# The gate projection as seven half-size products, summed in DRAM, beside the heads of an encoder layer

## The chip, the cores and the metric

The kernel runs on one core of a Trainium2 chip. The metric is the device time of one execution in microseconds (us). Three executions of the kernel before gave a median of 1530.08 us (1529.75 to 1530.29).

## The reference, cut to what matters

One layer with S = 1024 rows and D = 1024 columns. The heads, the pooling branch and the gates all read the same normalized input h:

```python
h = rmsnorm(x, g_mix[l])
z = h @ w_in[l]                      # pooling channels | q | k | v
...
qn = head_rmsnorm(q, g_q) * (HEAD_DIM ** -0.5)
kn = head_rmsnorm(k, g_k)
s = jnp.einsum('bqhid,bkhid->bihqk', qblk, kn)
...
gates = jax.nn.sigmoid(h @ w_gate[l] + b_gate[l])        # 1024 x 2048
merged = (gates[..., :D_MODEL] * (y_pool @ w_branch_pool[l])
          + gates[..., D_MODEL:] * (y_attn @ w_branch_attn[l]))
x = x + merged @ w_out[l]
h2 = rmsnorm(x, g_ffn[l])
x = x + jnp.square(jax.nn.relu(h2 @ w_up[l])) @ w_down[l]
```

## The kernel before, in words

Every float32 operand of a large product is split into a high and a low part (`split`: ScalarE makes the high part at L131, VectorE or GpSimd the low part at L132), and each product is three matmuls (`mm3`, L138 to L140: high by high, high by low, low by high). The transposed input hT lies in SBUF as four pairs of 128-row blocks (kp) by two halves of the rows (th) by high and low: sixteen tiles of 128 x 1024 words, in the pools `hp0` (th 0) and `hp1` (th 1).

The heads run as a software pipeline over 64 steps g (8 heads of 8 row blocks). The string `O` gives the stages and their lag in steps: A projects q, k and v (`stage_qkv`, 24 matmuls 128 x 384 into z), B normalizes q and k (`stage_prep`: ScalarE squares, VectorE sums, GpSimd raises to -1/2 at L271, VectorE scales, and GpSimd multiplies k's half by the weights `ggh` at L710), C transposes q and k and splits them (`stage_qkT`), D makes the scores and the softmax (`stage_scores`), E transposes the probabilities (`stage_aT`), F multiplies by v (`stage_pv`), H sums squares (`stage_ssq`), R writes the norms of a finished head to `r_dram` (`stage_norm`, L884), and W loads and splits the next head's weights `wqkv` (eight tiles, each free only when the old head's last block has used it).

TensorE's idle places in this pipeline are filled with *units* of other work, which `fillers` yields: a unit is half a column block (th) of the gates (`gate_cols`, 24 matmuls 128 x 512 into g, `fill_proj`) or of the pooling channels. One unit is traced for every two steps (`F_PACE` 0.5) from step 4 on, 34 of them in the loop and the last 6 behind it. Weights for the units go through two landing tiles `fr` and four split tiles `fw`; a gate unit's result gets its bias on ScalarE (L387) and is written to `g_dram` from ScalarE's queue (256 KB).

The order on each engine's queue is fixed when the program is built: a planner goes through the traced instructions by priority (tracing order) and by its own cost estimates, and an instruction waits on its engine until all its operands are there, with everything behind it on that engine waiting too. `tc.issue_after` holds an instruction behind another one of the same queue.

Behind the heads, stage `bp` multiplies the pooled rows by `w_branch_pool` (192 matmuls; its operands ypT lie in the `hp0` tiles that hT leaves), and stage `ba` multiplies the head outputs yT by `w_branch_attn` (384 matmuls). yT is loaded from `y_dram` and scaled by the rows of `r_dram`, so its last block needs the last head's norm. During `bp` `w_out_sums` also reads 4 MB of w_out and writes 4 MB of sums (`wos`, `w_sum`), in tiles whose room the heads' pool leaves. `gate` (L229, L230) then loads the gates and applies the sigmoid.

Of the kernel before, what the change touches and what calls it, by code (L numbers as in the profile page):

```python
# [48 lines left out]
ORDER = [(w[0], int(w[1:])) for w in O.split()]  # L49
G_FIRST, G_Z = 13, 13  # L50
F_FROM, F_PACE, F_UNITS = 4, 0.5, 34

# [11 lines left out]
def encoder_kernel(  # L64
# [86 lines left out]
    def w_tile(shape, name, i, dt=F32R):  # L151
        return wpool.tile(shape, dt, tag=f"W{int(i)}", name=name, bufs=N_W // 2)

    def fw_tile(shape, name, dt=F32R):
        return fwpool.tile(shape, dt, tag="fw", name=name)

    def fo_tile(name):
        return fp.tile([P, 528], F32, tag="fo", name=name, bufs=N_FO)
# [68 lines left out]
    def gate(gts, c):  # L227
        for gt, c0, c1 in gts:
            nc.sync.dma_start(gt, g_dram[c * P : (c + 1) * P, c0:c1])  # L229
            nc.scalar.activation(gt, gt, AF.Sigmoid, bias=zero)  # L230

# [32 lines left out]
    p_dram = dram.tile([POOLD, S], F32, name="p_dram")  # L264
    g_dram = dram.tile([2 * D, S], F32, name="g_dram")
    yd = dram.tile([S, D], F32, name="yd")

    def rsq(dst, ss, n, c):

        nc.vector.tensor_scalar(dst, ss, c, EPS, op0=ALU.mult, op1=ALU.add)  # L270
        nc.gpsimd.tensor_tensor(dst, dst, mhalf[:, :n], op=ALU.pow)  # L271

# [20 lines left out]
    h_hi = {}  # L293

    @contextmanager
    def first_gates(c):
        with tc.issue_after(h_hi[c + 2].ins), tc.issue_after(loads["x3"].ins):
            yield

# [80 lines left out]

    def gate_cols(c):
        with first_gates(c) if c < 3 else nullcontext():
            ws = fill_w(w_gate, c * P, f"gate{c}")
        for th in range(2):
            ps = fill_proj(ws, th, f"g{c}_{th}", spare_bank if c >= G_Z else fill_bank)
            fo = fo_tile(f"go{c}_{th}")
            nc.scalar.activation(fo[:, 0:512], ps, AF.Identity, bias=cols[:, c : c + 1])  # L387
            nc.scalar.dma_start(g_dram[c * P : (c + 1) * P, th * 512 : (th + 1) * 512], fo[:, 0:512])
            yield

    def gates():
        for c in range(2 * NK - 2):
            yield from gate_cols(c)
        for gen in [gate_cols(c) for c in (2 * NK - 2, 2 * NK - 1)] * 2:
            next(gen)
            yield

    def fillers():
        gate_units = gates()
        for _ in range(G_FIRST):  # L400
            next(gate_units)
            yield
        for g in range(4):
            for _ in pool_group(g):
                yield
                next(gate_units)
                yield
        for _ in gate_units:
            yield

    with ExitStack() as ph:
# [101 lines left out]

        gg = sp.tile([P, HD], F32, name="gg")
        hT.update(alloc_T(htile, "hT", 0))
# [96 lines left out]
        h1.append(turn(1, 1))  # L614
        q(dve.scalar_tensor_tensor, gg, gqk[:, 0, :], HD ** -0.5, gqk[:, 1, :], op0=ALU.mult, op1=ALU.mult)
        split_h(1, 1, h1[0])
# [31 lines left out]
        def columns():  # L648
            cols_ps = ps_t.tile([P, 512], F32, tag="tr", name="cols_ps")
            nc.tensor.transpose(cols_ps[:, 0:32], rows, identf[0:32, 0:32])  # L650
            nc.vector.tensor_copy(cols, cols_ps[:, 0:32])
            nc.vector.tensor_scalar(gs, cols[:, 20:21], 1.0 - LAMBDA_INIT, None, op0=ALU.mult)

# [19 lines left out]
        def head_start(h):  # L673
            gghs[h] = sp.tile([P, HD], F32, tag="ggh", name=f"ggh{h}", bufs=2)
            with behind():
                nc.gpsimd.tensor_scalar(gghs[h], gg, -(2.0 ** (h + 1)), None, op0=ALU.mult)
# [16 lines left out]
        def stage_prep(h, t):  # L693
            th = t // 4
            V, ggh = KV[h][1], gghs[h]
            z = st[h, t]["z"]
# [12 lines left out]
            )  # L709
            nc.gpsimd.tensor_tensor(  # L710
                qn[:, 2:4, :], qn[:, 2:4, :], ggh.unsqueeze(1).broadcast_to([P, 2, HD]), op=ALU.mult
            )
            st[h, t] = {"qn": qn}
            yield

        def stage_qkT(h, t):

            th, c0 = t // 4, (t % 4) * P
            K = KV[h][0][th]
            tr = ps_t.tile([P, 512], F32, tag="tr", name=f"tk{h}_{t}")  # L720
# [10 lines left out]
            for m in range(2):  # L731
                own, other = halves[m], halves[1 - m]
                q, k = tr[own, 0 : 2 * P], tr[own, 2 * P : 4 * P]
                k_hi, q_hi = K[own, m, c0:c1], Q[own, m, 0, :]
                nc.scalar.copy(k_hi, k)
                nc.vector.tensor_tensor(K[other, m, c0:c1], k, f(k_hi), op=ALU.subtract)
                nc.scalar.copy(q_hi, q)
# [180 lines left out]
        for g in range(-2, N + 10):  # L918
# [21 lines left out]
            while made < F_UNITS and made < (g - F_FROM) * F_PACE:  # L940
                next(units)
                made += 1
        for _ in units:
# [675 lines left out]
```

## Time and profile before

| | |
|---|---|
| median of three executions | 1530.08 us |
| span of the profiled execution, first to last instruction | 1526.9 us (the page gives no other time for it) |
| TensorE, busy share | 99% |
| VectorE, ScalarE, GpSimd | 67%, 52%, 26% |
| granted TensorE clock | 1.000 |
| gate matmuls | 768 (128 x 512), start to start 0.227 us when back to back |
| heads, branches and output projection, MLP | about 0 to 690, 690 to 920, 920 to 1527 us |

The busy time of a matmul in the profile (0.389 us for 128 x 512) overlaps its neighbours'. What a matmul costs TensorE is the distance from start to start.

### The profile page before, as it was taken

What the parts mean: (1) busy time and instruction counts of PE and PEld (TensorE: products, weight loads), DVE (VectorE), ACT (ScalarE), POOL (GpSimd) and SP (SyncE); (2) the same over time, 40 slices, a digit from 0 to 9 for tenths busy, and PEclk for the clock granted to TensorE, in tenths of its full rate; (3) what the DMA queues carried; (4) which work ended last, traced back from release to release, by engine and by line L of the source; (5) the groups of instructions that cost most, each with busy time, mean ns of one, the idle gap of its engine ahead of it and who ended that gap; (6) DMA issues with size and microseconds to landing.
All of it is one profiled execution on the core that took longest, in us unless ns stands there. A gap on an engine that the chain in (4) does not pass through costs nothing.

```text
span 1526.9 us, 21743 instructions
## 1 busy us (share of the span) xinstructions
PE 1517.4 (99%) x7637; PEld 1316.2 (86%) x7637; DVE 1025.5 (67%) x2135; ACT 794.6 (52%) x1653; POOL 389.4 (26%) x466
## 2 busy tenths in 40 slices
PE   9999999999999999999999999999999999999999
PEld 8899999999999999888888887888888788888887
DVE  7877766677777777742645899676656678556672
ACT  6655555556555555544633467565555634333331
POOL 5525242434334352318646510000000000000000
PEclk9999999999999999999999999999999999999999
DMA  6212111111202021339745633554433899537650
GB/s 213 66 48 66 34 53 52 59 51 39 73 31 80 33 87 49 118 106 376 269 139 174 212 138 117 173 195 156 152 124 111 290 333 367 182 125 260 229 191 28
DMA packets 168583, 213.75 MB, mean 140 GB/s; under 512 B 10165, under 2 KB 104090, under 8 KB 168474
## 3 DMA queue, kind: packets, MB, share of 16 engines
q1 hardware_dynamic: 151050, 185.05, 36.4%
q10 hardware_dynamic: 17424, 27.31, 4.9%
q8 instruction: 60, 0.98, 0.3%
q14 instruction: 49, 0.40, 0.1%
HBM read 154.62 MB, written 57.70 MB: 139 GB/s over the span
## 4 chain that ended last, share of the span: by engine, by line
PE 96%; DVE 2%; DMA 1%; ACT 1%; issue 0%; SPq 0%; POOLq 0%; POOL 0%; ACTq 0%; DVEq 0%
PE z L138 6%; PE z L139 5%; PE z L140 5%; PE Da L139 4%; PE Da L140 4%; PE Da L138 4%; PE g L138 4%; PE g L139 4%; PE g L140 4%; PE Db L138 3%; PE Db L139 3%; PE Db L140 3%; PE X L138 3%; PE X L139 3%; PE X L140 3%; PE sc L767 2%
## 5 line engine op out<-in xcount | busy, mean ns | idle before, releaser
L138 PE MATMUL z<-wqkv,hT 128*128 128x384 f32 x512 | 173.7, 340 | 1.2 <-ACT hT L131 1.1
L140 PE MATMUL z<-wqkv,hT 128*128 128x384 f32 x512 | 173.6, 339 | 0.4 <-DVE hT L437 0.3
L139 PE MATMUL z<-wqkv,hT 128*128 128x384 f32 x512 | 173.2, 338 | 0.0
L778 ACT ACTIVATE s<-s,nm 128x256 f32<-128x256 f32 (+7 forms) x128 | 99.5, 778 | 77.6 <-DVE nm L770 74.3
L271 POOL TENSOR_TENSOR ms<-ms,mhalf 128x4 f32<-128x4 f32 x64 | 66.7, 1042 | 186.8 <-DVE ms L270 183.3
L138 PE MATMUL g<-hT,fwgate 128*128 128x512 f32 x256 | 101.0, 395 | 0.0
L139 PE MATMUL g<-hT,fwgate 128*128 128x512 f32 x256 | 100.5, 392 | 0.0
L140 PE MATMUL g<-hT,fwgate 128*128 128x512 f32 x256 | 100.4, 393 | 0.0
L138 PEld LDWEIGHTS z<-wqkv,hT 128*128 128x128 f32 x512 | 96.2, 188 | 4.0 <-ACT hT L131 1.2
L140 PEld LDWEIGHTS z<-wqkv,hT 128*128 128x128 f32 x512 | 96.2, 188 | 2.6 <-DVE hT L437 0.9
L139 PEld LDWEIGHTS z<-wqkv,hT 128*128 128x128 f32 x512 | 96.3, 188 | 2.4 <-DVE wqkv L437 0.3
L770 DVE CUSTOM_DVE_ANT_0 s<-sc,dist 128x512 f32<-128x512 f32 (+3 forms) x128 | 74.1, 585 | 21.2 <-PE sc L768 20.3
L767 PE MATMUL sc<-K,Q 128*128 128x512 f32 (+2 forms) x192 | 67.5, 357 | 0.4 <-DVE nm L770 0.4
L768 PE MATMUL sc<-K,Q 128*128 128x512 f32 (+2 forms) x192 | 66.1, 349 | 0.0
L132 DVE TENSOR_TENSOR AS<-s,AS 128x512 fp32r<-128x512 f32 x64 | 43.4, 687 | 30.9 <-ACT AS L131 30.9
L132 POOL TENSOR_TENSOR wqkv<-rqkv,wqkv 128x384 fp32r<-128x384 f32 x56 | 58.7, 1065 | 14.6 <-ACT wqkv L131 14.2
L132 POOL TENSOR_TENSOR fwgate<-frgate,fwgate 128x512 fp32r<-128x512 f32 x32 | 43.5, 1361 | 66.0 <-ACT fwgate L131 66.0
L140 PEld LDWEIGHTS g<-hT,fwgate 128*128 128x128 f32 x256 | 48.1, 188 | 9.5
L138 PEld LDWEIGHTS g<-hT,fwgate 128*128 128x128 f32 x256 | 48.1, 188 | 9.1 <-ACT go L387 0.2
L139 PEld LDWEIGHTS g<-hT,fwgate 128*128 128x128 f32 x256 | 48.1, 188 | 8.8
L132 DVE TENSOR_TENSOR AT_0l<-ta,AT_0h 128x512 fp32r<-128x512 f32 (+1 forms) x48 | 32.0, 666 | 32.0 <-ACT AT_0h L131 31.7
L139 PE MATMUL ba<-yT,wba 128*128 128x512 f32 x128 | 49.6, 389 | 0.0
(481 smaller groups left out, 4625.9 us busy)
## 6 DMA issues: line engine op xcount, KB each, us to landing
wd<-in_w_down_dram SPq DMA_DIRECT2D x56, 512.0 KB, 5.4
wu<-in_w_up_dram SPq DMA_DIRECT2D x32, 512.0 KB, 4.3
udS<-us SPq DMA_DIRECT2D x64, 256.0 KB, 3.3
ur<-udS SPq DMA_DIRECT2D x32, 512.0 KB, 4.5
rqkv<-in_w_in_dram SPq DMA_DIRECT2D x64, 192.0 KB, 3.0
ur<-ud SPq DMA_DIRECT2D x24, 512.0 KB, 6.4
frgate<-in_w_gate_dram SPq DMA_DIRECT2D x32, 256.0 KB, 3.6
g_dram<-go ACTq DMA_DIRECT2D x32, 256.0 KB, 3.2
```

Source lines behind the costliest of these rows:

```text
L132: (lo_eng or nc.vector).tensor_tensor(lo, src, f(hi), op=ALU.subtract)
L138: nc.tensor.matmul(ps, lhs_hi, rhs_hi, start=first, stop=False, **kw)
L139: nc.tensor.matmul(ps, lhs_hi, rhs_lo, start=False, stop=False, **kw)
L140: return nc.tensor.matmul(ps, lhs_lo, rhs_hi, start=False, stop=last, **kw)
L271: nc.gpsimd.tensor_tensor(dst, dst, mhalf[:, :n], op=ALU.pow)
L767: nc.tensor.matmul(dst, Q[:, i, 0, :], rhs, start=True, stop=False)
L768: nc.tensor.matmul(dst, Q[:, i, 1, :], rhs, start=False, stop=True)
L770: nc.vector.tensor_tensor_reduce(out=s[i][:, c : c + w], in0=sc[:, 0:w], in1=dist[:, o0 + c : o0 + c + w], scale=2.0 ** -(h + 1), scalar=B ...
L778: nc.scalar.activation(s[i][:, 0:n], s[i][:, 0:n], AF.Exp, bias=last, scale=-1.0, accum_out=Z[:, i, t : t + 1])
```

## The change

The gates' product H W, with H cut into 2 x 2 quarters (rows by inner dimension, 512 x 512) and W into 2 x 2 (inner dimension by branch, 512 x 1024), is made by Strassen's scheme in Winograd's form: seven products of half the size in place of eight. A product of one 128-column block is 12 matmuls, so 56 products take 672 matmuls.

- Sums of W's quarters are made in DRAM: a plain transfer copies a quarter or an earlier sum (SyncE's queue, 2 MB), and an accumulating transfer from GpSimd's queue adds another quarter to it (`gate_sums`, four sums `gw_sum`).
- The rows' quarters are put together in DRAM too (`h_dram`: high part copied, low part added). Their differences T5, T6, T4, T7 are loaded, subtracted on GpSimd and split (`t_set`), into the tiles `fu` and `mx` of the pooling groups and two of the four `fw` tiles (new tag `fT`), so that two `fw` tiles are left while the T sets are in use.
- A product (`gate_product`) is copied out of PSUM by ScalarE and added by an accumulating transfer from GpSimd's queue to one, two or three of the four quarters `gd[c]` of the result; product 1 writes all four with a plain transfer from ScalarE's queue.
- `G_PLAN` is the order of the units; a product counts one, a pooling unit two; one is traced a step (`F_PACE` 1.0), 60 in the loop, so to step 64, and 12 products behind it. `G_SUMS` puts the transfers between them.
- `gate` loads from `gd` and adds the bias with the sigmoid (the second branch with the opposite sign).
- The weights of q and k no longer go over GpSimd: the column `gcol` (one transpose) times -2^(h+1) is the scale of ScalarE's copy and of VectorE's subtraction of K in `stage_qkT`.

```diff
-F_FROM, F_PACE, F_UNITS = 4, 0.5, 34
+F_FROM, F_PACE, F_UNITS, F_SPARE = 4, 1.0, 60, 58
+G_PLAN = "1 1 1 1 U 1 U 1 U 1 U 1 2 2 2 2 2 2 2 2 3 3 t5 3 5 5 5 5 5 5 5 5 t6 3 3 6 6 6 6 6 6 6 6 t4 3 3 4 4 4 4 4 4 4 4 t7 3 7 7 7 7 7 7 7 7"
+G_SUMS = {3: "h0", 5: "c1", 6: "h1", 8: "a1", 10: "h2", 11: "c2", 12: "c3", 13: "h3", 15: "a2", 17: "a3", 18: "c4", 20: "a4"}
+G_TO = {"1": (0, 4), "6": (1, 4), "7": (2, 4), "5": (1, 3), "2": (0, 1), "3": (1, 2), "4": (3, 4)}
...
+    def gate_product(j, c):
...
+            marks["SP"] = nc.sync.dma_start(rw, src[r0 : r0 + 512, c0 : c0 + P].rearrange("(kk p) c -> p kk c", p=P)).ins
+            w = fw_tile([P, 2, 4, P], f"fwg{j}_{c}")
+            split(w[:, 0], w[:, 1], rw, nc.gpsimd)
+        ps = (spare_bank if n >= F_SPARE - 16 else fill_bank)(f"g{j}_{c}")
+        for k in range(4):
+            if j in "123":
+                b = [hT[k // 2 + 2 * (j != "1"), int(j == "3"), hl][:, k % 2, :] for hl in range(2)]
+            else:
+                b = pair(T[j, k])
+            mm3(ps, w[:, 0, k, :], w[:, 1, k, :], *b, k == 0, k == 3)
+        fo = fo_tile(f"go{j}_{c}")
...
+        q0, q1 = G_TO[j]
+        dst = gd[c][q0:q1].rearrange("q p t -> p q t")
+        from_ = fo[:, 0:512].unsqueeze(1).broadcast_to([P, q1 - q0, 512])
+        if j == "1":
+            nc.scalar.dma_start(dst, from_)
+        else:
+            nc.gpsimd.dma_start(dst, from_, accum_op=ALU.add)
...
+    def t_set(j):
...
+        for k in range(4):
...
+            rw = raw([P, S], f"rT{j}_{k}")
+            a, b = rw[:, 0:512], rw[:, 512:S]
...
+                nc.gpsimd.tensor_tensor(a, a, b, op=ALU.subtract)
...
+            split(hi, lo, a, nc.gpsimd)
+        if j == "5":
+            nc.gpsimd.dma_start(t2_dram, h_dram[1][1], accum_op=ALU.add, max_dma_last_dim=1024)
...
-            nc.gpsimd.tensor_tensor(
-                qn[:, 2:4, :], qn[:, 2:4, :], ggh.unsqueeze(1).broadcast_to([P, 2, HD]), op=ALU.mult
-            )
...
-                nc.scalar.copy(k_hi, k)
-                nc.vector.tensor_tensor(K[other, m, c0:c1], k, f(k_hi), op=ALU.subtract)
+                g = gghs[h][own]
+                nc.scalar.activation(k_hi, k, AF.Copy, scale=g)
+                nc.vector.scalar_tensor_tensor(K[other, m, c0:c1], k, g, f(k_hi), op0=ALU.mult, op1=ALU.subtract)
```

More of the change, by code (lines that the diff above doesn't have):

```diff
@@ L152, in w_tile @@
         return wpool.tile(shape, dt, tag=f"W{int(i)}", name=name, bufs=N_W // 2)
+    fwcount, fw_all = [0], [True]
     def fw_tile(shape, name, dt=F32R):
-        return fwpool.tile(shape, dt, tag="fw", name=name)
+        n = fwcount[0]
+        fwcount[0] += 1
+        return fwpool.tile(shape, dt, tag="fT" if fw_all[0] and n // 2 % 2 else "fw", name=name, bufs=N_FW // 2)
     def fo_tile(name):
@@ L228, in gate @@
         for gt, c0, c1 in gts:
-            nc.sync.dma_start(gt, g_dram[c * P : (c + 1) * P, c0:c1])
-            nc.scalar.activation(gt, gt, AF.Sigmoid, bias=zero)
+            for th in range(c0 // 512, c1 // 512):
+                nc.sync.dma_start(gt[:, th * 512 - c0 : th * 512 - c0 + 512], gd[c % NK][th if c < NK else 3 - th])
+            nc.scalar.activation(gt, gt, AF.Sigmoid, bias=cols[:, c : c + 1], scale=1.0 if c < NK else -1.0)
     def whole(g):
@@ L379, in pool_group @@
             nc.scalar.dma_start(p_dram[g * P : (g + 1) * P, th * 512 : (th + 1) * 512], yp[:, 0:512])
[L381 to L389, printed above, removed]
@@ new lines, in fillers @@
+    def fillers():
+        turn, step, groups = {}, 0, 0
+        for w in G_PLAN.split():
+            if w[0] == "t":
+                fw_all[0] = False
+                t_set(w[1])
+                continue
+            if step in G_SUMS:
+                gate_sums(G_SUMS[step])
+            step += 1
+            if w == "U":
+                for _ in pool_group(groups):
+                    yield 2
+                groups += 1
+            else:
+                gate_product(w, turn.setdefault(w, 0))
+                turn[w] += 1
+                yield 1
+        fw_all[0] = True
+        fwcount[0] = 0
@@ L694, in stage_prep @@
             th = t // 4
-            V, ggh = KV[h][1], gghs[h]
+            V = KV[h][1]
             z = st[h, t]["z"]
@@ L718, in stage_qkT @@
             th, c0 = t // 4, (t % 4) * P
+            if t == 0:
+                gghs[h] = sp.tile([P, 1], F32, tag="ggh", name=f"ggh{h}", bufs=2)
+                nc.gpsimd.tensor_scalar(gghs[h], gcol, -(2.0 ** (h + 1)), None, op0=ALU.mult)
             K = KV[h][0][th]
```

105 lines of the change are left out of this document (74 added, 31 removed).

## The prediction

> **What bounds the kernel now.** I read the page first, then the windows, then single groups.
>
> ```profile
> span 1526.9 us, 21743 instructions
> PE 1517.4 (99%) x7637; PEld 1316.2 (86%) x7637; DVE 1025.5 (67%) x2135; ACT 794.6 (52%) x1653; POOL 389.4 (26%) x466
> ...
> PE 96%; DVE 2%; DMA 1%; ACT 1%; issue 0%; SPq 0%; POOLq 0%; POOL 0%; ACTq 0%; DVEq 0%
> ...
> 100.00:560.00 460.00, 460.00 (x2687) 426.52 (x2686) 332.06 (x1000) 264.27 (x685) 180.85 (x248) 1.00 0.18 55
> 620.00:690.00 70.00, 69.55 (x355) 58.78 (x354) 36.07 (x97) 34.66 (x70) 15.30 (x16) 1.00 0.33 110
> 690.00:740.00 50.00, 50.00 (x222) 41.40 (x221) 19.91 (x20) 23.32 (x42) 40.61 (x30) 1.00 1.04 387
> ```
>
> TensorE is busy throughout, and the chain that ended last is 96% TensorE. The three windows (busy us of PE, PEld, DVE, ACT, POOL, then clock, DMA share, GB/s) are the heads, their drain, and stage `bp`: TensorE is full in all, GpSimd has 61% to spare in the heads, the DMA engines idle in the heads but are saturated in `bp` (1.04). So matmuls taken away count in full, unless something else becomes late. The span is 3.2 us under the median, 1530.08; I sum against the span and add 3.2.
>
> **What a gate matmul costs.**
>
> ```profile
> L138 PE MATMUL g<-hT,fwgate 128*128 128x512 f32 x256 | 101.0, 395 | 0.0
> L138 PE MATMUL bp<-ypT,wbp x64: 389/389/389, 695.9 to 738.8; 128*128 128x512 f32 x64
> 620.00:696.00 76.00, 61.77 (x258) 1.00 0.38 129
> ```
>
> The first row suggests 0.395 us each, or 37.9 us for the 96 matmuls that go (768 to 672). But durations overlap: the same shape in `bp`, back to back, has 63 intervals of three matmuls between 695.9 and 738.8, 0.227 us each. So 96 x 0.227 = 21.8 us go. The Trainium skill, "TensorE: Matmul & The Clock Gate", Back-to-back issue gap, gives about 131 ns a matmul of 512 columns in a sustained stream; by it the estimate would be 96 x 0.131 = 12.6 us and the time 1522.5. The trace does not agree (0.227), and I go by the trace.
>
> Where they go: per step the units bring 12 matmuls before (24 every two steps) and after (12 each). What vanishes is units 31 to 34, behind step 64, in the drain: the third row counts 258 gate matmuls between 620 and 696, and 162 remain.
>
> **What is added, step by step.**
>
> ```profile
> L132 POOL TENSOR_TENSOR fwgate<-frgate,fwgate 128x512 fp32r<-128x512 f32 x32 | 43.5, 1361 | 66.0 <-ACT fwgate L131 66.0
> L710 POOL TENSOR_TENSOR qn<-qn,ggh 128x128 f32<-128x128 f32 x64 | 35.4, 553 | 55.5 <-DVE qn L704 46.3 <-DVE ms L270 5.3 <-DVE cf L785 2.4
> L878 POOL TENSOR_TENSOR r<-r,mhalf 128x8 f32<-128x8 f32 x8 | 13.1, 1637 | 44.3 <-DVE r L877 44.3
> L387 ACT ACTIVATE go<-g,cols 128x512 f32<-128x512 f32 x32 | 21.9, 688 | 25.9 <-PE g L140 25.4 <-ACT oqs L131 0.2
> L131 ACT CAST fwgate<-frgate 128x512 fp32r<-128x512 f32 x32 | 19.7, 619 | 7.6 <-PE g L140 6.5 <-PE u L140 0.9
> ...
> L736 DVE TENSOR_TENSOR K<-tk,K x64: 417/422/428, 48.0 to 630.1; 64x256 fp32r<-64x256 f32 x64
> ...
> g_dram<-go ACTq DMA_DIRECT2D x32, 256.0 KB, 3.2
> ```
>
> *TensorE*: one transpose for `gcol`, 0.3 us at most.
>
> *GpSimd*: low parts of weights 32 to 56, +24 x 1.36 = 32.7 us; the T sets, 12 subtractions and 16 low parts of the same shape, 28 x 1.36 = 38.1; the k multiplication goes, -35.4. New are 61 accumulating issues: 48 products, 8 for `h_dram`, 4 for the weight sums, 1 for T2. No row shows one. Below: an issue on ScalarE's queue takes 0.29 us (the `r_dram` row further down); above: the transfer's whole landing, 3.2 us, if the engine were held so long. It is work of GpSimd itself, nearest to its short operations, 0.55 to 1.64 us; I take 1.3, so 79 us. GpSimd gains 115 us, in 600 us of heads: from 39% to near 60%. No bound on average.
>
> *ScalarE*: 24 more copies out (0.688, 16.5 us) and 40 more high parts (0.619, 24.8): 57% to 64%. K's copy with a scale instead of a plain one, and VectorE's subtraction with a factor (0.42 us before): a few hundredths each, off the path.
>
> *Transfers*: the gates moved 8 MB of weights and 8 MB of results. Now: 14 MB of weights, 8 MB plain results, 80 accumulated quarters (20 MB), 16 MB of weight sums, some 12 MB for h and T. 54 MB more over 600 us are 90 GB/s on top of 55, where `bp` shows 387 moved. Even at double cost for accumulation there is room. SyncE issues about 76 transfers more at 0.3 to 0.5 us; its queue's own waits are the price, below.
>
> *The wait inside a unit*: two `fw` tiles mean that a product's weights (0.62 + 1.36 = 2.0 us) are split while the one before runs (12 x 0.227 = 2.7 us). One a step, this is covered. The T sets: each first tile needs the last product of the old set, then subtraction done, 0.62 + 1.36 us; all four take GpSimd 11 us. One or two products 3 and a step's q, k, v matmuls lie between. Bounds 0 to 5 us each; the plan leaves a step or more for most, so 1 each: 4 us.
>
> *Head boundaries*, the tightest place on GpSimd:
>
> ```profile
> 299.00:309.00 10.00, 10.00 (x54) 8.93 (x53) 8.78 (x21) 4.98 (x13) 8.43 (x10) 1.00 0.42 124
> 305.08 2.43 POOL L132 TENSOR_TENSOR wqkv<-rqkv,wqkv 128x384 fp32r<-128x384 f32 x2
> 309.46 0.33 PE L139 MATMUL z<-wqkv,hT 128*128 128x384 f32 x1
> L132 POOL TENSOR_TENSOR wqkv<-rqkv,wqkv x56: 1004/1017/1478, 64.3 to 544.8; 128x384 fp32r<-128x384 f32 x56
> ```
>
> GpSimd is busy 8.4 of 10 us, and the last weights are ready at 307.5, 2.0 us before TensorE reads them. The change puts 1.3 (issue) + 0.7 (half a split) there and takes 0.55 + 0.4 (`ggh`) away: +1.1, within the 2.0. I take 1 us in all; the bound above is in the third rival.
>
> **The drain and `bp`**, where the gain must come out.
>
> ```profile
> L140 PE MATMUL z<-wqkv,hT x48: 334/334/343, 563.6 to 616.2; 128*128 128x384 f32 x48
> 654.16 0.39 PE L767 MATMUL sc<-K,Q 128*128 128x512 f32 x1
> 658.65 1.29 DVE L787 SCALAR_TENSOR_TENSOR s<-s,cf,s 128x1024 f32<-128x1024 f32 x1
> 663.75 1.04 PE L823 MATMUL ta<-identf,s 128*128 128x128 f32 x8
> 665.61 0.68 DVE L132 TENSOR_TENSOR AT_4l<-ta,AT_4h 128x512 fp32r<-128x512 f32 x1
> 669.20 0.28 PE L138 MATMUL po<-AT_0h,V 128*128 128x256 f32 x1
> 673.95 0.42 DVE L132 TENSOR_TENSOR oqs<-oq,oqs 128x256 fp32r<-128x256 f32 x1 [7.65 <-ACT oqs L131]
> 678.23 0.28 PE L860 MATMUL po<-oqs,ones 128*128 128x256 f32 x1
> 681.81 0.35 POOL L879 TENSOR_TENSOR r<-r,rz 128x8 f32<-128x8 f32 x1
> 686.47 0.27 PE L881 MATMUL trr<-identf,r 128*8 128x128 f32 x1
> 687.14 0.29 ACTq L884 DMA_DIRECT2D r_dram<-rT  x1
> L138 PE MATMUL ba<-yT,wba x90: 389/389/389, 739.4 to 800.0; 128*128 128x512 f32 x90
> L132 DVE TENSOR_TENSOR yT<-ryT,yT x12: 678/868/1781, 695.0 to 744.8; 128x512 fp32r<-128x512 f32 x12
> ```
>
> The last q, k, v matmul is at 616, the last norms leave at 687, then come 52 us of saturated transfers, and `ba` starts at 739 while its last yT is split only at 745: transfers and TensorE finish together. So to start `ba` 21.8 us earlier, the norms must leave by 665, 49 us behind the last z instead of 71. The rows show where the last head waits for TensorE's order: the softmax is done at 659.9 and transposed at 663.8 (3.8 us), split at 666.3 and multiplied by v from 669.2 (2.9), squared at 674.4 and summed at 678.2 (3.9), its norm ready at 682.2 and transposed at 686.5 (4.3). In those 14.9 us TensorE runs gate units. With four units fewer, and all others traced behind the loop, the planner has less to put between; the other 7 us would come from the scores between 616 and 654. The pooled rows also get their tiles (`hp0`) earlier, since the late products 7 read T and not hT, so `bp` can fill TensorE in the drain. Taken: 0; bounds 0 (it all comes forward) and 21.8 (nothing does).
>
> **Sum.** 1526.9 - 21.8 + 0.3 + 4 + 1 = 1510.4 us of span, + 3.2: 1513.6 us.
>
> **Rivals.**
>
> *The transfers do not come forward.* The norms still leave 60 to 71 us behind the last z, or the 20 accumulated quarters of the 12 late products (5 MB; 13 us at 387 GB/s) push into the saturated 52 us. Then `ba` waits, with TensorE idle just ahead of it for 7 to 20 us: 1520 to 1533. For it: the DMA share of 1.04 and the yT row. Against: at 620 to 690 the share is 0.33, and the late products fall there.
>
> *More than the matmuls.* The k multiplication left a chain of the step, and TensorE's 9.5 us of idle time could shrink; at most 1504. Against: nearly all that idle time is outside the heads.
>
> *Slower: the accumulating issues hold up GpSimd.* Its queue is in order, so an issue that waits for its copy, or takes long, delays the weight splits and L271 behind it, and z and the transposes of q and k wait. At the seven head boundaries a price x per issue costs x - 0.2 - 2.0 us each once the slack is gone; the 16.5 us that are forecast are lost at x = 4.6 us. At 6 us: 7 x 3.8 = 27, so 1540; at 10 us, 1568. For it: no row bounds such an issue, and 8.4 of 10 us. Against: 3.2 us is the whole landing of a 256 KB store. The Trainium skill, "SBUF — State Buffer", Who interferes with whom, says that a VectorE instruction with two SBUF inputs and a GpSimd one that reads SBUF shut each other out. The rule leans the way of this rival; the spread of the `wqkv` splits (1004 to 1478 ns) fits it, at half a microsecond, which moves no chance.
>
> **How the numbers follow.** Forecast 0.53 (own range 1506 to 1520), transfers late 0.27, more than the matmuls 0.04, slower by GpSimd 0.16. A measurement tells 0.2% (3 us) from no change. Faster by more than that: 0.53 + 0.04 + two thirds of 0.27 = 0.74; same 0.10; slower 0.16. The range for 8 in 10 leaves out the rival below and most of GpSimd's: 1505 to 1533.
>
> **What would show it.** Right: 672 gate matmuls; TensorE without waits in the heads; `r_dram`'s last store near 50 us behind the last z; `ba` starting near 720 without idle time ahead of it. Wrong: TensorE waiting on `wqkv` or on T's low parts; GpSimd's accumulating issues of 3 us and more in its rows, or L271 late; an idle stretch ahead of `ba` with the DMA share at 1; the clock below 1.000.

## The result, and the profile after

The changed kernel takes 1573.28 us (median of four; 1573.15 to 1573.71), the kernel before 1530.18 us beside it. The ratio is 1.0283, 95% interval 1.0268 to 1.0297: 43 us slower, where 16.5 us faster was forecast.

The page of the changed kernel first: span and busy time, the DMA queues, the chain that ended last.

```profile
span 1571.4 us, 21898 instructions
PE 1520.1 (97%) x7542; PEld 1309.3 (83%) x7542; DVE 1075.2 (68%) x2137; ACT 831.0 (53%) x1717; POOL 487.7 (31%) x515
...
q0 software_dynamic: 16336, 34.61, 14.2%
...
PE 73%; DMA 9%; DVE 8%; POOL 3%; ACT 3%; issue 3%; SPq 1%; POOLq 0%; ACTq 0%; DVEq 0%
```

TensorE runs 95 instructions fewer (96 matmuls less, one transpose more) and is busy *longer*, 1520 us against 1517, and now other engines and transfers take a quarter of the chain where it was 4%. Queue q0, which GpSimd fills, is new. The windows say where:

```profile
30.00:100.00 70.00, 64.17 (x359) 57.50 (x358) 52.55 (x141) 44.13 (x118) 33.28 (x41) 1.00 0.63 190
100.00:560.00 460.00, 444.67 (x2536) 407.54 (x2535) 339.68 (x950) 267.13 (x671) 209.29 (x245) 0.98 0.58 134
560.00:680.00 120.00, 112.36 (x634) 102.18 (x633) 85.29 (x236) 72.49 (x182) 67.41 (x72) 0.99 0.61 128
680.00:780.00 100.00, 89.32 (x405) 72.61 (x403) 50.78 (x79) 49.69 (x98) 71.82 (x57) 0.97 0.98 286
```

TensorE (second number) no longer fills any window: 6 us are lost before 100, 15 in 100 to 560, where it was busy 460.00 of 460.00 before, 8 and 11 behind. The DMA share there went from 0.18 to 0.58 for 134 GB/s in place of 55. And the clock, 1.00 throughout before, is below 1 in three of the four. Most of the longer busy time comes from there. Three pairs of windows, a stall first and the stretch behind it second:

```profile
392.50:399.00 6.50, 3.77 (x23) 3.41 (x21) 0.22 (x1) 0.00 (x0) 0.00 (x0) 1.00 0.61 110
399.30:406.00 6.70, 4.71 (x13) 4.23 (x14) 2.78 (x9) 5.26 (x14) 3.95 (x4) 0.50 0.51 153
...
597.00:600.50 3.50, 1.92 (x11) 1.47 (x9) 0.20 (x1) 2.14 (x6) 0.00 (x0) 1.00 0.61 154
604.00:607.40 3.40, 3.13 (x10) 3.06 (x11) 3.32 (x12) 1.50 (x4) 1.37 (x2) 0.50 0.02 5
...
774.70:781.50 6.80, 4.94 (x22) 3.68 (x21) 6.80 (x5) 3.77 (x7) 6.80 (x4) 1.00 1.02 413
781.50:788.30 6.80, 4.56 (x12) 3.27 (x11) 6.80 (x5) 2.41 (x3) 6.64 (x5) 0.50 0.79 283
```

Behind these stalls the granted clock is 0.50 for 3.4 or 6.8 us. There are seven such pieces up to 790 us, 34 us in all, and TensorE is busy in 28 of them: by an estimate some 14 us of work are lost, so a stall can be paid for a second time. Not every stall is: behind 2.6 us at 50 and 2.3 us at 576 the clock stays at 1.00. (The Trainium skill, "TensorE: Matmul & The Clock Gate", What's actually happening, gives half speed after an idle window of about 3.4 us. The pieces are one or two times that length, but three of them follow stretches of 2.2 to 3.2 us in which TensorE was idle.)

Three stalls show what kind of thing happens. The one at 396 us is a late sum of weights: its last accumulating transfer was issued at 381.3 and took 16.4 us to land, the load behind it started at 397.7, and TensorE was idle for 5.0 us until the weights were split (ScalarE's row):

```profile
400.62 0.62 ACT L133 CAST fwg<-frg 128x512 fp32r<-128x512 f32 x1 [8.41 <-DMA frg<-gw_sum]
```

The second: first GpSimd, then VectorE, then TensorE, about 600 us (start, length, instruction; in brackets the idle time before and what ended it):

```profile
590.07 2.26 POOL L134 TENSOR_TENSOR fwg<-frg,fwg 128x512 fp32r<-128x512 f32 x1
601.12 1.26 POOL L439 TENSOR_TENSOR rT<-rT 128x512 f32<-128x512 f32 x1 [8.79 <-DMA rT<-h_dram]
602.32 0.34 POOL L908 MEMSET AT<- 128x128 f32 x2
602.62 1.04 POOL L283 TENSOR_TENSOR ms<-ms,mhalf 128x4 f32<-128x4 f32 x1
...
603.70 0.42 DVE L801 TENSOR_TENSOR qn<-z,ms 128x256 f32<-128x256 f32 x1 [6.50 <-POOL ms L283]
...
604.27 0.66 PE L140 MATMUL z<-wqkv,hT 128*128 128x384 f32 x1 [5.35 <-DVE qn L801]
```

T's subtraction (L439) stands at the head of GpSimd's queue and waits 8.8 us for its load; behind it waits the power for q and k's norm (L283, L271 before), then VectorE, then TensorE.

The third, first GpSimd, then VectorE:

```profile
569.77 1.31 POOL L483 DMA_DIRECT2D gd<-go  x1
570.60 0.70 POOL L908 MEMSET AT_0h<- 128x128 f32 x1
570.75 0.70 POOL L908 MEMSET AT_0l<- 128x128 f32 x1
570.91 0.69 POOL L977 TENSOR_TENSOR r<-r,rz 128x8 f32<-128x8 f32 x1
571.08 1.78 POOL L134 TENSOR_TENSOR fwg<-frg,fwg 128x512 fp32r<-128x512 f32 x1
572.33 4.37 POOL L134 TENSOR_TENSOR wqkv<-rqkv,wqkv 128x384 fp32r<-128x384 f32 x4
...
570.90 6.22 DVE L885 SCALAR_TENSOR_TENSOR s<-s,cf 128x384 f32<-128x384 f32 x1
577.05 0.68 DVE L868 CUSTOM_DVE_ANT_0 s<-sc,dist 128x512 f32<-128x512 f32 x1
```

Here one VectorE instruction, 0.6 us for this shape elsewhere, lasts 6.22 us: from the issue of a transfer on GpSimd (L483) to the end of the unbroken run behind it. Both its inputs are in SBUF.

### The profile page after: what moved, and what is told of

Read it like the earlier page. It is cut to its first block, busy times and chain, and to the rows that moved or that the text cites. A ratio compares the mean times of both kernels' runs of the same rounds, so it can differ in the third digit from the quotient of the medians.

```text
span 1571.4 us, 21898 instructions
## 1 busy us (share of the span) xinstructions
PE 1520.1 (97%) x7542; PEld 1309.3 (83%) x7542; DVE 1075.2 (68%) x2137; ACT 831.0 (53%) x1717; POOL 487.7 (31%) x515
## 4 chain that ended last, share of the span: by engine, by line
PE 73%; DMA 9%; DVE 8%; POOL 3%; ACT 3%; issue 3%; SPq 1%; POOLq 0%; ACTq 0%; DVEq 0%
PE z L140 4%; PE z L141 4%; PE z L142 4%; PE Da L141 4%; PE Da L142 4%; PE Da L140 4%; PE Db L142 3%; PE Db L141 3%; PE Db L140 3%; PE X L140 3%; PE X L142 2%; PE X L141 2%; PE g L140 2%; PE g L141 2%; PE g L142 2%
## 5 line engine op out<-in xcount | busy, mean ns | idle before, releaser
L140 PE MATMUL z<-wqkv,hT 128*128 128x384 f32 x512 | 176.6, 345 | 7.1 <-DVE qn L801 6.1
L141 PE MATMUL z<-wqkv,hT 128*128 128x384 f32 x512 | 175.6, 343 | 0.0
L142 PE MATMUL z<-wqkv,hT 128*128 128x384 f32 x512 | 175.3, 343 | 0.0
L283 POOL TENSOR_TENSOR ms<-ms,mhalf 128x4 f32<-128x4 f32 x64 | 68.1, 1064 | 143.5 <-DVE ms L282 140.7
L140 PEld LDWEIGHTS z<-wqkv,hT 128*128 128x128 f32 x512 | 97.8, 191 | 11.8 <-issue 5.7
L141 PEld LDWEIGHTS z<-wqkv,hT 128*128 128x128 f32 x512 | 97.7, 191 | 3.9 <-POOL wqkv L134 0.4
L142 PEld LDWEIGHTS z<-wqkv,hT 128*128 128x128 f32 x512 | 97.5, 191 | 2.8 <-DVE hT L531 0.5
L134 POOL TENSOR_TENSOR fwg<-frg,fwg 128x512 fp32r<-128x512 f32 x56 | 90.1, 1610 | 25.5 <-ACT fwg L133 25.5
L483 POOL DMA_DIRECT2D gd<-go x48 | 54.6, 1138 | 44.3 <-ACT go L476 26.2
L140 PE MATMUL g<-T,fwg 128*128 128x512 f32 x128 | 51.6, 404 | 3.6 <-ACT fwg L133 3.6
L141 PE MATMUL ba<-yT,wba 128*128 128x512 f32 x128 | 50.7, 397 | 4.1 <-DVE yT L134 4.1
L142 PE MATMUL g<-T,fwg 128*128 128x512 f32 x128 | 51.7, 404 | 0.7 <-POOL fwg L134 0.7
L801 DVE TENSOR_TENSOR qn<-z,ms 128x256 f32<-128x256 f32 x64 | 26.9, 420 | 37.2 <-POOL ms L283 22.2
L141 PE MATMUL g<-T,fwg 128*128 128x512 f32 x128 | 51.2, 400 | 0.0
L142 PE MATMUL ba<-yT,wba 128*128 128x512 f32 x128 | 50.5, 395 | 0.0
L921 PE MATMUL ta<-identf,s 128*128 128x128 f32 x288 | 45.4, 276 | 4.9 <-DVE s L885 3.2
## 6 DMA issues: line engine op xcount, KB each, us to landing
gw_sum<-in_w_gate_dram POOLq DMA_DIRECT2D x4, 2048.0 KB, 16.1
```

The costliest lines, as they stand in the source:

```text
L134: (lo_eng or nc.vector).tensor_tensor(lo, src, f(hi), op=ALU.subtract)
L140: nc.tensor.matmul(ps, lhs_hi, rhs_hi, start=first, stop=False, **kw)
L141: nc.tensor.matmul(ps, lhs_hi, rhs_lo, start=False, stop=False, **kw)
L142: return nc.tensor.matmul(ps, lhs_lo, rhs_hi, start=False, stop=last, **kw)
L283: marks["POOL"] = nc.gpsimd.tensor_tensor(dst, dst, mhalf[:, :n], op=ALU.pow).ins
L483: nc.gpsimd.dma_start(dst, from_, accum_op=ALU.add)
```

## The experiments

Each time is a median; the kernel before took 1529.6 to 1530.2 beside them. Intervals are those of the ratio to the kernel before.

**The matmuls alone** (`b_less`): the kernel before, 96 gate matmuls fewer.

```diff
-F_FROM, F_PACE, F_UNITS = 4, 0.5, 34
+F_FROM, F_PACE, F_UNITS = 4, 0.5, 30
...
-        for gen in [gate_cols(c) for c in (2 * NK - 2, 2 * NK - 1)] * 2:
```

> The kernel before, with its last four gate units left out (96 matmuls; two column blocks of the gates are read from their neighbours), nothing else changed: what the matmuls alone are worth. By the prediction's step it takes 96 x 0.227 = 21.8 us off, so 1508 us. If the transfers of the drain do not come forward it gives 1515 to 1530. Either way it says how much of the 43 us of loss stands against a gain that was there.

1510.6 us, ratio 0.9869 (0.9853 to 0.9886): 20 us. So the gain was there to be had, the drain lets nearly all of it out (1508 was expected), and the changed kernel loses 62.7 us (1573.3 - 1510.6) against it.

**The keys' weights alone** (`b_k`): the kernel before with `gcol` and the scaled key copy.

```diff
-            nc.gpsimd.tensor_tensor(
-                qn[:, 2:4, :], qn[:, 2:4, :], ggh.unsqueeze(1).broadcast_to([P, 2, HD]), op=ALU.mult
...
+                nc.scalar.activation(k_hi, k, AF.Copy, scale=g)
```

> The kernel before with the second part of the change alone: k's weights as the scale of the key copies, GpSimd's multiplication gone. Theory: this part is harmless, 1528 to 1532 us. Rival: the scaled copy and the subtraction with a factor lengthen the chain from the transposes to the scores, and the loss is partly here: over 1535 us.

1531.7 us, ratio 1.0008 (0.9999 to 1.0017). Harmless.

**Parts left out of the changed kernel, one at a time, and all together.** `e_plain` stores the products without accumulation, `e_noT` drops T and the rows' sums, `e_nosum` the weight sums, `e_bare` all three.

```diff
 e_plain
-            nc.gpsimd.dma_start(dst, from_, accum_op=ALU.add)
+            nc.gpsimd.dma_start(dst, from_)
 e_noT
-                t_set(w[1])
...
-            if j in "123":
+            if True:
 e_nosum (products 3, 6 and 7 likewise; the transfers of the sums go)
-"5": (gw_sum["1"], 0, c0)
+"5": (w_gate, 0, c0)
```

> The changed kernel with the 48 accumulating transfers of the products made plain stores of the same shape from the same queue (the gates are then wrong numbers); T sets, sums of weights and rows stay. If the accumulating transfers hold up the loads beside them (T's loads landed 12 us after their issue at 589 us), those loads land earlier and most stalls go: 1535 to 1550 us. If GpSimd's queue and its elementwise work are the cause, the time stays within 5 us of 1573.

> The changed kernel without the T sets and without the sums of the rows in DRAM: products 4 to 7 read hT instead of T (wrong gates); the weight sums and the accumulating products stay. The two kernels measured so far put 38 us of the loss on the transfers and T (1573 against 1535 for the kernel without any of them). Theory, GpSimd's queue held by the T loads and its 28 added instructions: most of it goes here, 1545 to 1553 us; the stalls at 598 and 701 us go, and those at 30 to 60 us as well, if the sums of the rows cause them. Rival, the accumulating transfers of the products and the weight sums are the larger part: 1560 us or more.

> The changed kernel without the weight sums (products 3, 5, 6 and 7 read w_gate directly; wrong gates): 16 MB less is moved, T sets and accumulating products stay. If the late sum at 396 us (TensorE 5.0 us idle and then 6.8 us at half clock) is the whole harm, 1563 to 1567 us. If 2 MB transfers also hold up the loads beside them elsewhere: 1550 to 1560.

> The changed kernel with its products stored plainly, the sums of weights and of rows left out (all products read w_gate and hT directly, no T sets): 56 products of 12 matmuls and 56 splits on GpSimd stay, so does the order of the units. The gates are then wrong numbers. If the loss comes from the transfers and from GpSimd's queue behind them, the matmuls' gain shows: 1508 to 1520 us. If it comes from the added GpSimd work on the weights (VectorE and GpSimd in each other's way) or from the pooling units packed into steps 9 to 30, most of the loss stays: 1545 us or more.

| left out | us | off 1573.3 | ratio to before, interval |
|---|---|---|---|
| accumulation (`e_plain`) | 1557.1 | 16.2 | 1.0165 (1.0141 to 1.0190) |
| T and row sums (`e_noT`) | 1556.9 | 16.4 | 1.0171 (1.0155 to 1.0187) |
| weight sums (`e_nosum`) | 1566.7 | 6.6 | 1.0239 (1.0221 to 1.0257) |
| all three (`e_bare`) | 1535.2 | 38.1 | 1.0033 (1.0020 to 1.0046) |

The three add up to 39.2, and all together take 38.1. The other 25 us, 1535 against 1511, lie in what `e_bare` keeps. Only `e_nosum` came as the first theory had it; `e_bare`, `e_plain` and `e_noT` fell between what the theories expected, so none of the three parts is the cause alone. One of the prices is cleaner than the others: in the traces `e_plain` and the changed kernel have the same instructions in the same order on every engine, so its 16.2 us are accumulation's alone. In `e_noT`, `e_nosum` and `e_bare` the planner has put the queues in another order, and that is in their prices too.

**Order, and work moved to VectorE.** `e_spread` draws the four pooling units apart; `e_fwdve` makes the weights' low parts on VectorE.

```diff
 e_spread
-"1 1 1 1 U 1 U 1 U 1 U 1 2 2 2 2 2 2 2 2 3 3 t5
+"1 1 1 1 U 1 1 U 1 1 2 U 2 2 2 U 2 2 2 2 3 3 t5
 e_fwdve
-            split(w[:, 0], w[:, 1], rw, nc.gpsimd)
+            split(w[:, 0], w[:, 1], rw)
```

> The changed kernel with one edit to the order of the units: the four pooling units stand two or three products apart up to the sixteenth product, not one product apart. Nothing else changes, and the gates are right. If VectorE's density between 200 and 330 us (80% busy) makes the scores wait there, those stalls (some 12 us with their half clock) shrink: 1560 to 1567 us. If the stalls come from single VectorE instructions shut out by GpSimd, they only move: 1570 to 1576.

> The changed kernel with one edit: the low parts of the 56 gate weights are made by VectorE (0.68 us each for this shape) and not by GpSimd (1.6 us each). The gates are right. If VectorE instructions shut out by GpSimd's elementwise runs are the main cause, the excess goes and the time falls to 1550 to 1562 us. If VectorE's own load is the cause (38 us more on an engine at 75% in the heads), it rises: 1578 us or more.

`e_spread` 1581.5 us (1.0320 to 1.0351), 8 slower; `e_fwdve` 1573.8 (1.0263 to 1.0297), no change. Both are outside what either theory expected: neither VectorE's density beside the pooling units nor GpSimd's splits of the gate weights by themselves explain the loss. And `e_spread` says how far a mere change of order moves this kernel: nearly every edit makes the planner order the queues anew, so differences of a few us between variants of the changed kernel can't be assigned to their edit alone.

**Is it GpSimd's work?** `b_pool` doubles low parts in the kernel before, `b_burst` puts four runs of 12 subtractions into it, `e_Tsb` makes T in the changed kernel from SBUF, without loads and without the rows' sums (T6, which was loaded as it is, becomes a copy by GpSimd).

```diff
 b_pool, after each split of weights
+            nc.gpsimd.tensor_tensor(w[:, 1], rw, f(w[:, 0]), op=ALU.subtract)
...
 b_burst, at gate columns 4, 6, 8 and 10
+            for i in range(12):
+                nc.gpsimd.tensor_tensor(
+                    o, f(hT[i % 4, 0, 0][:, i % 2, :]), f(hT[i % 4, 1, 0][:, i % 2, :]), op=ALU.subtract
+                )
 e_Tsb
-                nc.sync.dma_start(a, sa[rows, :])
-                nc.sync.dma_start(b, sb[rows, :])
-                nc.gpsimd.tensor_tensor(a, a, b, op=ALU.subtract)
+                nc.gpsimd.tensor_tensor(
+                    a, f(hT[k // 2 + sa[0], sa[1], 0][:, k % 2, :]), f(hT[k // 2 + sb[0], sb[1], 0][:, k % 2, :]),
+                    op=ALU.subtract,
+                )
```

> The kernel before, in which GpSimd makes each low part of the weights of the gates and of the pooling units twice, the same instruction with the same result: 40 more instructions 128x512, some 54 us more of GpSimd's elementwise work in the heads, without any transfer, T set or change of the units. If such work by itself shuts VectorE out and delays the chain, 1535 us or more. If GpSimd's work is harmless as long as no instruction of its queue waits for a transfer, 1528 to 1532 us.

> The kernel before with four runs of 12 GpSimd subtractions 128x512 in a row, hT from hT, into the free tiles of the pooling groups (their result is not used): 48 instructions, 63 us, much like the 40 spread ones that cost 1.7 us. If an unbroken run shuts VectorE's instructions with two SBUF inputs out until it ends, each run costs TensorE several us: 1540 to 1565 us, with VectorE instructions of 5 us and more beside the runs. If only the amount counts: 1530 to 1534.

> The changed kernel with the T sets made from hT's high parts in SBUF (the low parts are left out of T, and T5 of the sum behind T6 and T4, so the gates are wrong): the same GpSimd subtractions and splits in the same places, but no sums of the rows in DRAM, no T loads. The kernel without T sets took 1557 us, the changed one 1573. If the loads that GpSimd's queue waits for and the sums beside them are the cause, it stands near the first: 1555 to 1562. If the 28 instructions themselves are: 1568 to 1576.

`b_pool` 1531.3 us (1.0002 to 1.0021) and `b_burst` 1534.7 (1.0019 to 1.0041): 54 and 63 us more of GpSimd's work cost 2 and 5 us. In `b_burst` GpSimd's runs reach 52 us without a gap, and still the coefficient cf of the softmax, 0.2 us on VectorE, lasts at most 1.3 us. So neither the amount of GpSimd's work nor an unbroken run is enough. And `e_Tsb`, 1583.1 us (1.0332 to 1.0363), is *slower* by 10 us without the loads that GpSimd's queue had waited for, more than either theory expected, so those waits are not the whole cause either. Its timeline at 687 us, first GpSimd, then VectorE:

```profile
685.38 2.83 POOL L134 TENSOR_TENSOR T<-rT,T 128x512 fp32r<-128x512 f32 x2
687.88 1.57 POOL L435 TENSOR_TENSOR rT<-hT,hT 128x512 f32<-128x512 f32 x1
689.12 1.17 POOL L478 DMA_DIRECT2D gd<-go  x1
...
694.02 2.14 POOL L134 TENSOR_TENSOR fwg<-frg,fwg 128x512 fp32r<-128x512 f32 x1
...
687.48 8.71 DVE L879 SCALAR_TENSOR_TENSOR cf<-cf,Z,nlam 128x1 f32<-128x1 f32 x1
696.11 0.28 DVE L134 TENSOR_TENSOR AT<-ta,AT 128x128 fp32r<-128x128 f32 x1
```

An instruction on one column, 0.2 us otherwise, lasts 8.71 us, as long as GpSimd's run, which has issues of transfers in it. That is what the runs of `b_burst` lack, and it made the next pair.

**T by VectorE** (`e_Tsb_dve` from SBUF, `e_tdve` as loaded).

```diff
-                nc.gpsimd.tensor_tensor(a, a, b, op=ALU.subtract)
+                nc.vector.tensor_tensor(a, a, b, op=ALU.subtract)
-            split(hi, lo, a, nc.gpsimd)
+            split(hi, lo, a)
```

> The kernel with T made from hT in SBUF (1583 us), with T's subtractions and low parts on VectorE (0.7 us each) and not on GpSimd (1.3 to 1.8 us). If the runs on GpSimd cost the time, it falls to 1553 to 1563 us, near the kernel without T (1557). If the T sets cost by being late for their first product whoever makes them: 1572 or more.

> The changed kernel, T loaded from DRAM as it is there, with T's subtractions and low parts on VectorE; the gates are right. VectorE's queue now waits for the T loads (8 to 10 us at 590 us) where GpSimd's did. If the wait for the loads at a queue's head is a cause of its own, nothing is gained or it gets worse: 1570 to 1590 us. If only GpSimd's runs matter: 1558 to 1565.

1572.1 (1.0258 to 1.0288) and 1575.9 us (1.0287 to 1.0330). Without loads, VectorE saves 11 us on `e_Tsb`, but not the 26 to `e_noT`; with loads nothing is gained, as expected if VectorE's queue then waits where GpSimd's did.

**No transfer issued by GpSimd** (`e_noswq`), and **only such issues** (`b_gpdma`).

```diff
 e_noswq (also the sums of weights and rows, as plain copies from SyncE's queue)
-        if j == "1":
-            nc.scalar.dma_start(dst, from_)
-        else:
-            nc.gpsimd.dma_start(dst, from_, accum_op=ALU.add)
+        nc.scalar.dma_start(dst, from_)
 b_gpdma
-            nc.scalar.dma_start(g_dram[c * P : (c + 1) * P, th * 512 : (th + 1) * 512], fo[:, 0:512])
+            nc.gpsimd.dma_start(g_dram[c * P : (c + 1) * P, th * 512 : (th + 1) * 512], fo[:, 0:512])
```

> The changed kernel with no transfer issued by GpSimd: product stores plain from ScalarE's queue, the weight and row sums replaced by plain copies from SyncE's queue (gates wrong, T and the sums then hold one addend); T sets, their loads and subtractions, the order of the units stay. To be read against the kernel with plain stores from GpSimd's queue, 1557 us. If GpSimd's issues stretch VectorE's instructions, none is stretched by over 1.3 us here, and the time falls to 1538 to 1550 us. If they are harmless: 1552 to 1560 us.

> The kernel before with one word changed: the 32 stores of the gates (256 KB each, plain) are issued by GpSimd and not by ScalarE. If a transfer issued by GpSimd keeps VectorE's two-input instructions out until GpSimd's run behind it ends, VectorE instructions 1.5 us and more over their form's least time appear, which this kernel never had, and the time rises by 2 to 10 us. If the stretched instructions come from something else in the changed kernel (T, the sums, the wide stores): none appears, 1528 to 1532 us.

`e_noswq` takes 1536.0 us (1.0029 to 1.0061), somewhat less than the theory said, 21 less than `e_plain` and 37 less than the changed kernel, with T sets, their loads and the bytes moved all kept. Beside GpSimd's issues it differs from `e_plain` in two things: the 13 accumulating transfers of the sums are plain copies there, and the engines' queues are in another order. The rows of the coefficient and of the scaling of s in the changed kernel, in `e_plain`, and in `e_noswq` (least, median and longest duration in ns):

```profile
L884 DVE SCALAR_TENSOR_TENSOR cf<-cf,Z,nlam x64: 200/220/4079, 67.6 to 708.0; 128x1 f32<-128x1 f32 x64
L885 DVE SCALAR_TENSOR_TENSOR s<-s,cf x32: 336/545/6223, 67.8 to 660.2; 128x128 f32<-128x128 f32 x8, 128x256 f32<-128x256 f32 x8, 128x384 f32<-128x384 f32 x8, 128x512 f32<-128x512 f32 x8
```

```profile
L884 DVE SCALAR_TENSOR_TENSOR cf<-cf,Z,nlam x64: 200/220/3877, 67.0 to 696.9; 128x1 f32<-128x1 f32 x64
DMA packets 201177, 275.63 MB, mean 177 GB/s; under 512 B 11973, under 2 KB 119210, under 8 KB 201002
q0 software_dynamic: 11216, 34.61, 8.7%
```

```profile
L878 DVE SCALAR_TENSOR_TENSOR cf<-cf,Z,nlam x64: 206/220/1050, 64.2 to 681.7; 128x1 f32<-128x1 f32 x64
L879 DVE SCALAR_TENSOR_TENSOR s<-s,cf x32: 342/542/1660, 64.5 to 631.9; 128x128 f32<-128x128 f32 x8, 128x256 f32<-128x256 f32 x8, 128x384 f32<-128x384 f32 x8, 128x512 f32<-128x512 f32 x8
DMA packets 205288, 275.62 MB, mean 180 GB/s; under 512 B 11973, under 2 KB 118186, under 8 KB 205098
```

The same median, the same 275.6 MB; only the long ones are gone, and queue q0 with them. Over the traces of all kernels: of the nine without transfers issued by GpSimd in the heads, or with those of `b_gpdma` alone, none has a VectorE instruction between 20 and 930 us that lasts over 1.3 us more than the least of its form; of the eleven others each has 5 to 15 that exceed theirs by more than 1.5 us (13 in the changed kernel, 39 us together), all within 4.5 us behind the start of such an issue. But `b_gpdma`, 1530.4 us (0.9996 to 1.0013), has 32 plain issues and none of these. An issue alone does not do it; what else it takes (a longer run of GpSimd behind it, sums, wider stores) stays open. Nor do the long instructions by themselves set the time: `e_fwdve` has 5 of them, 14 us together in place of 39, and is no faster, and `e_bare_old` below has 5 and loses about 1 us in the heads.

**What `e_bare` keeps.** `e_bare_old` puts the pooling units back to their old places, `e_bare_narrow` makes each product's store 256 KB from ScalarE's queue, `e_bare_all` does both with four weight tiles throughout.

```diff
 e_bare_old: G_PLAN with 26 products, then U among every four
 e_bare_narrow
+        nc.scalar.dma_start(gd[c][q0], fo[:, 0:512])
 e_bare_all
-tag="fT" if fw_all[0] and n // 2 % 2 else "fw"
+tag="fT" if n // 2 % 2 else "fw"
```

> The kernel without sums, T sets and accumulation (1535 us), with the pooling units where the kernel before had them: 26 products first, then one pooling unit among every four products. If the packing of the pooling units into steps 9 to 30 is what the heads lose there (TensorE's losses between 150 and 350 us were 12 us above the kernel before), 1522 to 1527 us. If the added splits and the single-bank order are: 1533 to 1538.

> The kernel without sums, T sets and accumulation (1535 us), each product now stored once (256 KB) from ScalarE's queue: no 1 MB stores, no transfer issued by GpSimd in the heads. If the wide stores and their issue on GpSimd still cost time in that kernel: 1522 to 1530 us, above all from the drain, where transfers share the engines with the loads of the branches. If they do not: 1533 to 1537.

> The kernel without sums, T sets and accumulation, with the pooling units in their old places (1529 us), one narrow store for each product from ScalarE's queue, and four weight tiles throughout. The two single edits were worth 5.8 and 3.8 us on 1535; with both and the tiles 1518 to 1526 us if they add up; near 1511 if the drain's waits go as well; 1527 or more if the drain is set by something else, such as 56 products with a weight split and a copy-out each in place of 28.

1529.4 (0.9989 to 1.0008), 1531.4 (1.0004 to 1.0023) and 1517.0 us (0.9901 to 0.9930): 5.8, 3.8 and 18.2 us off 1535.2. The first two fell between what their theories expected; the third is 8.6 us more than the two together, so the four tiles, or all three edits at once, are worth something too. The heads of `e_bare_old` lose about 1 us against the kernel before (TensorE busy 458.95 of 460 us from 100 to 560); what is left is in the drain, where the last head's norm is late. First GpSimd, then TensorE:

```profile
699.29 2.50 POOL L134 TENSOR_TENSOR wba<-rba,wba 128x512 fp32r<-128x512 f32 x2 [4.31 <-DVE r L972]
701.89 2.11 POOL L975 TENSOR_TENSOR r<-r,mhalf 128x8 f32<-128x8 f32 x1
703.98 1.26 POOL L134 TENSOR_TENSOR wba<-rba,wba 128x512 fp32r<-128x512 f32 x1
705.21 0.19 POOL L976 TENSOR_TENSOR r<-r,rz 128x8 f32<-128x8 f32 x1
...
705.45 0.38 PE L978 MATMUL trr<-identf,r 128*8 128x128 f32 x1 [5.73 <-POOL r L976]
```

Low parts of the next stage's weights stand between the steps of the norm in GpSimd's queue, and TensorE waits 5.7 us. With narrow stores and four tiles too, the kernel is within 6.4 us of `b_less`.

The account of the 62.7 us between `b_less` and the changed kernel: 16 accumulation of the products (to `e_plain`); 21 GpSimd's issues, the 13 accumulating sums and a new order together (to `e_noswq`); 25 that remain. Nearly as much remains in `e_bare`, where 18 went with the order of the units, the wide stores on GpSimd's queue and the tiles. That those 18 lie in the 25 of `e_noswq` too is not shown, since GpSimd issues nothing there already. And the issues alone may be worth much less than 21: taking GpSimd's 48 plain issues out of `e_bare`, with narrower stores, gave 3.8 us (`e_bare_narrow`). No version that keeps all the sums came near the kernel before; `e_noswq` has plain copies in their place.

## Why the prediction was wrong, point by point

- **Matmuls, 21.8 us: right.** 20 us (17.4 to 22.5 by the interval), so the spacing of the trace held. The 12.6 us by the Trainium skill lie outside it (they would have made 1522.8 us, not 1522.5).
- **Drain, 0 us: nearly right for the matmuls alone, by a wrong step, and wrong for the change.** I required that the norms leave 49 us behind the last z, by 665. In `b_less` the last transpose of the norms runs at 690.6 and `ba` starts at 720.5:

```profile
L879 PE MATMUL trr<-identf,r x8: 270/271/273, 150.7 to 690.6; 128*8 128x128 f32 x8
L138 PE MATMUL ba<-yT,wba x128: 389/389/389, 720.5 to 806.9; 128*128 128x512 f32 x128
```

  Later norms and an earlier `ba`: the 52 us between the two before were not a length that transfers needed. In the changed kernel the last norms left at 740.0, 79 us behind the last z (71 before, 49 forecast), and TensorE was idle for 10.7 us between 680 and 780, at a clock of 0.97. No term of the sum stood for that.
- **Keys' weights, about 0: right** (`b_k`).
- **The issue of an accumulating transfer, 1.3 us on GpSimd: right as a duration, wrong as a cost.** This is the first step that failed, as far as the runs tell. Measured:

```profile
L483 POOL DMA_DIRECT2D gd<-go x48 | 54.6, 1138 | 44.3 <-ACT go L476 26.2 <-PE sc L866 6.3 <-PE ta L921 5.7
L439 POOL TENSOR_TENSOR rT<-rT 128x512 f32<-128x512 f32 x12 | 17.2, 1434 | 16.5 <-DMA rT<-h_dram 16.4
```

  1.14 us each, near enough. But "No bound on average" looked at GpSimd's time alone. Issuing these transfers elsewhere, with the sums plain, gives 21 us back at the same bytes; how much of that is the issues is not shown. I had the rule in hand, the Trainium skill's "SBUF — State Buffer", Who interferes with whom, and gave it "half a microsecond, which moves no chance", since the row of the `wqkv` splits showed no more. Where GpSimd issues no transfers that is still so, at most 1.3 us, about one instruction of GpSimd's; here one instruction took up to 6.2 us. The same skill's "DMA: Bandwidth & Descriptors", SWDGE vs HWDGE vs iDMA, says that GpSimd builds the descriptors of its transfers in SBUF itself, where VectorE can lock it out in its two-port modes, that transfers issued by SyncE or ScalarE are free of that interference, and that accumulation is only to be had from GpSimd. What the runs show is the other direction, VectorE held up: not in `e_noswq`, and not in `b_gpdma` either, though GpSimd issues there.
- **Transfers, "Even at double cost for accumulation there is room": failed.** This is the step whose price is clean: 16.2 us for accumulation in the products, in an unchanged order. Bandwidth was there (share 0.58 in the heads; 62 MB more by the page, 54 forecast), but the landings got longer: those of the accumulating stores (KB, median us), then of the plain ones of `e_plain`:

```profile
gd<-go POOLq DMA_DIRECT2D x16, 512.0 KB, 7.8
gd<-go POOLq DMA_DIRECT2D x24, 256.0 KB, 4.3
```

```profile
gd<-go POOLq DMA_DIRECT2D x16, 512.0 KB, 4.8
gd<-go POOLq DMA_DIRECT2D x24, 256.0 KB, 2.5
L439 POOL TENSOR_TENSOR rT<-rT 128x512 f32<-128x512 f32 x12 | 15.8, 1323 | 5.4 <-DMA rT<-h_dram 4.0 <-issue 1.4
```

  Accumulation makes a landing 1.6 to 1.7 times as long (1.8 for the eight of 768 KB, 8.5 against 4.6), and GpSimd waits 16.4 us for T's loads, 4.0 without accumulation. Most of the difference is the one wait of 8.8 us that began at 592. As the order is the same, the two traces can be laid matmul by matmul: TensorE is 0.7 us behind `e_plain` at 467 us, 8.8 at 606, behind that stall, and 16.6 at 790. So about half of the 16 us is lost between 467 and 606, most of it at that stall, and the rest from 677 on, in the drain. That accumulation's longer landings make both is likely, but was not tried apart.
- **T sets, 4 us: mis-sized, 16.4 us** with the rows' sums and a new order (`e_noT`), though hardly for being built: with the transfers on other queues, T, the copies for both kinds of sum and the wider stores cost some 5 us (`e_noswq` 1536.0 against `e_bare_narrow` 1531.4, which has none of them and no issue of GpSimd's).
- **Not priced at all: the order and room of the units.** Pooling units packed into steps 9 to 30, stores of 512 KB to 1 MB, two weight tiles where four were, and GpSimd's queue for the stores: 18 us together (`e_bare` to `e_bare_all`). "One a step, this is covered" is in doubt for the tiles, but alone they were not tried. Nor was there a wait for the sums of the weights: TensorE waited 8.6 us in all for split gate weights, 5.0 of them at 396 for the late sum.
- **The rivals.** "Slower by GpSimd", with 0.16, named the engine and the direction. Its place (seven boundaries) and condition (4.6 us an issue) were not what decided. Of the signs listed for a wrong prediction, L271 (now L283) late and a clock below 1.000 came; issues of 3 us did not, and no wait of TensorE of half a microsecond ended with T's low parts or `wqkv`. "The transfers do not come forward", with 0.27, came in part: the norms were late, and TensorE waited 4.1 us for yT, not ahead of `ba` but just inside it, with the DMA share at 1.02.
- What stays open: how much of the 21 us is the stretched VectorE instructions and how much the plain landings of hardware queues (512 KB in 2.7 us in `e_noswq`, the one landing of 16 that its trace tells, 4.8 in `e_plain`, the median of 16), how much the sums made plain, and how much the new order, since `e_noswq` changes them all.

## What to carry to other kernels

A transfer is not priced by its bytes and its issue: ask whose queue issues it, who else has its two inputs in SBUF at that time, and which load at a queue's head lands behind it. Where a kernel's busiest engine has no idle time, work saved on it is worth its full price, but any chain that now passes a queue waiting for DRAM turns spare time into stalls, and here most stalls of 2 us and more were followed by 3.4 to 6.8 us at half clock. Before such a change is built whole, leave the matmuls out alone (20 us here) and put the transfers in alone; the second was not tried here but for plain stores (`b_gpdma`, no loss). And where a planner orders the queues, compare the order of two traces before an edit is given a price: here only `e_plain` kept it, and a mere change of the units' order moved the time by 8 us (`e_spread`).

## What the runs showed of the hardware that I had not expected

- A VectorE instruction with two SBUF inputs waited at most 1.3 us, about one GpSimd instruction, even beside a run of 52 us, but up to 8.7 us in kernels where GpSimd also issued transfers with sums or wide stores among them.
- GpSimd's issue took 0.70 us for a plain and 1.14 us for an accumulating store of the same shapes; a 2 MB accumulating transfer landed in 16.1 us.
- The granted clock fell to 0.50 in pieces of 3.4 or 6.8 us behind stalls of TensorE of 2 to 5 us, or several shorter ones, in a stream that was otherwise dense; two stalls of 2.3 and 2.6 us had no such piece behind them.
